# Weight tiles in two halves, read woven by the products of a two-layer hybrid encoder

## The chip, the cores and the metric

The kernel runs on one core of one Trainium2 chip. The metric is the device time of one execution in microseconds; the median of the runs is compared. Four engines matter here: TensorE (PE, its weight loads are called PEld), VectorE (DVE), ScalarE (ACT) and GpSimd (POOL). SyncE (SP) issues most of the DMA transfers.

## What is computed

Two layers act on 256 tokens of 2048 channels, all in float32. The reference, cut to what matters:

```python
def hybrid_layer(x, ...):
    h = rmsnorm(x, norm_g)
    proj = h @ w_in                                   # 2048 x 13376
    (c_a, c_glu, c_gate, q_down, kv_down, k_pe, m_gate, g_conv, g_mla) = jnp.split(proj, idx, axis=-1)
    # causal depthwise convolution of width 31, LayerNorm over channels, two gates
    y_conv = conv_branch(c_a, c_glu, c_gate, conv_w, conv_b, conv_ln_g, conv_ln_b) @ w_proj_conv
    # 16 heads, queries and keys from 512 latent channels, chunk-causal mask
    y_mla = mla_branch(q_down, kv_down, k_pe, m_gate, cos, sin, ..., w_uq, ..., w_ukv, ...) @ w_proj_mla
    y = jax.nn.sigmoid(g_conv) * y_conv + jax.nn.sigmoid(g_mla) * y_mla
    return x + y @ w_out
```

## The kernel before

**Products.** Every matrix product keeps a 128x128 block of the activations stationary in TensorE and lets a block of weights of up to 512 columns (384 or 320 for the low-rank inputs, `down`) move past it. For accuracy each float32 operand is split in two parts of the format fp32r, `hi` (rounded) and `lo` (the rest), and each product becomes three: activation `hi` by weight `hi`, activation `lo` by weight `hi`, activation `hi` by weight `lo`. The 256 tokens make two halves `t`, each with an accumulator `acc` in PSUM.

**Weight pieces.** The weights are cut into pieces of two blocks of 128 rows (`KS = 2`) by one block of columns. The host lays a piece out so that each partition has its two rows one after the other. SyncE loads a piece into `raw` (`load`, up to four pieces ahead), ScalarE copies it to `hi` (`split_hi`, three ahead), VectorE subtracts to get `lo` (`split_lo`, two ahead). The first two pieces of the program are loaded and split row by row. A full piece then serves twelve products of 512 columns: two rows, two halves of the tokens, three parts. `order_of_products` says in which order; `products_at_end` issues the last products of the program.

**Order.** `order_of_layer` lists the blocks of a layer: gated inputs of the convolution (`glu`), latent inputs (`down`), query and key/value products (`uq`, `ukv`) with the attention of eight pairs of heads between them, gates (`cgate`, `mgate`, `gmla`, `gconv`), the projections `pmla` and `pconv`, and `wout`. Each engine executes its instructions in the order in which the program issues them.

**The planner.** After each piece the program calls `background(n)`, which stands for one slot of time. The slot's length is a formula, and VectorE and ScalarE get a budget of it less the cost of the next split:

```python
slot = 12 * (n / 2400 + 0.0133) - 0.04
for e, split_us in (("vec", KS * n / 960 + 0.06), ("act", KS * n / 1066 + 0.04)):
    budget[e] = min(budget[e], 0.0) + slot - split_us
```

Evacuations of accumulators and attention steps come due at fixed slots and are charged. As long as VectorE's budget is positive, entries of the queue `fill` are issued: the 31 taps of the convolution for each of eight blocks (`conv`, tile `v_t`, running sum `s1c`), and then the LayerNorm (`mean`, `centre`, `var`, `factors`, `apply`) and the gating (`gated`), which yields `ycT`, the stationary operand of `pconv`. With budget left, ScalarE computes taps ahead (`assist`, tile `tap`). When `pconv` is reached, `run_fill` is called until `ycT` exists, and `before_pconv` forces each of its four parts before the pieces that use it.

Of the kernel before, what the change touches and what calls it, by code (L numbers as in the profile page):

```python
# [11 lines left out]
F32 = mybir.dt.float32  # L12
F32R = mybir.dt.float32r
# [6 lines left out]
P = 128  # L20
# [4 lines left out]
DEPTH = 2  # L25
# [32 lines left out]
R_QA, R_KVA, R_QR, R_KR, R_N = 0, LORA, 2 * LORA, 2 * LORA + ROPE, 2 * LORA + 2 * ROPE  # L58

KS = 2  # L60
N_WARM = 19


# [60 lines left out]
def trunk(ctx: ExitStack, tc: tile.TileContext, xT, x, g_in, pos, win, wuq, wukv, wpc, wpm, wo, cst, rows, invf, out):  # L124
# [19 lines left out]
    pe, vec, act, gps, sp = (InOrder(e) for e in (nc.tensor, nc.vector, nc.scalar, nc.gpsimd, nc.sync))  # L144
# [3 lines left out]
    raw_p = pool("raw", 5)  # L148
    split_p = pool("split", 3)
# [18 lines left out]
    pieces = []  # L168

    def plan(layer, stream):  # L170
        ap, nk = streams[stream]
        i, at = taken.get((layer, stream), (0, 0))
        n = blocks_of_layer()[stream][i]
        mine = []
        for g in range(nk // KS):
            size = P * KS * n
            pieces.append((ap[layer, at : at + size].rearrange("(p k c) -> p k c", p=P, k=KS), n))
            at += size
            mine.append(len(pieces) - 1)
        taken[layer, stream] = (i + 1, at)  # L180
        return nk, n, mine
# [6 lines left out]
    loaded, highs, done, blocks_begun = {}, {}, {}, [0]  # L188
    LOAD_AHEAD, HI_AHEAD, LO_AHEAD = 4, 3, 2

    def load(i):
        if i >= len(pieces) or i in loaded:
            return
        ap, n = pieces[i]
        loaded[i] = t = raw_p.tile([P, KS, n], F32, tag="raw", name=f"raw{i}")
        for a in range(0, KS, 1 if i < 2 else KS):
            k = slice(a, a + 1 if i < 2 else KS)
            sp.dma_start(t[:, k, :], ap[:, k, :])

    def split_hi(i):  # L200
        if i >= len(pieces) or i in highs:
            return
        load(i)
        highs[i] = split_p.tile([P, KS, pieces[i][1]], F32R, tag="hi", name=f"hi{i}", bufs=4)
        singly = i < 2
        for a in range(0, KS, 1 if singly else KS):
            k = slice(a, a + 1 if singly else KS)

            for step in ("h", "w"):
                if step == "w":  # L210
                    act.copy(highs[i][:, k], loaded[i][:, k])
                    if singly:
                        split_lo(i, k)
                elif i * KS < NCT:
                    for c in range(i * KS + k.start, i * KS + k.stop):
                        first_h(c)
        for a in range(1, LOAD_AHEAD + 1):
            load(i + a)

    def split_lo(i, k=slice(0, KS)):  # L220
        if i >= len(pieces) or done.get(i, (0, 0, 0))[2] >= k.stop:
            return
        lo = done[i][1] if i in done else split_p.tile([P, KS, pieces[i][1]], F32R, tag="lo", name=f"lo{i}")
        vec.tensor_sub(lo[:, k], loaded[i][:, k], highs[i][:, k].bitcast(F32))
        done[i] = highs[i], lo, k.stop


# [23 lines left out]

    def background(n):
        clock[0] += 1
        slot = 12 * (n / 2400 + 0.0133) - 0.04
        for e, split_us in (("vec", KS * n / 960 + 0.06), ("act", KS * n / 1066 + 0.04)):
            budget[e] = min(budget[e], 0.0) + slot - split_us
        while True:
            due = [e for e in steps if e[0] <= clock[0]]
            if not due:
                break  # L260
            steps[:] = [e for e in steps if e[0] > clock[0]]
            for _, costs, f in due:
                spend(costs)
                f()
            while early:
                early.pop(0)()
        while fill and budget["vec"] > 0:
            after, slots, scalar = fill[0][1]
            if after and clock[0] < marks.get(after, 1 << 30) + slots or scalar and budget["act"] < 0:
                break  # L270
            run_fill()

        while assist and budget["act"] > 0.8 and assist[0]():
            budget["act"] -= 0.85
        finish_late()
# [13 lines left out]
    def order_of_products(i, last, tardy):  # L289

        two = range(2)
        if i < 2:
            return [(t, kk, p) for kk in range(KS) for p in range(3) for t in two]
        high, low = (lambda t, p: [(t, kk, p) for kk in range(KS)]), (lambda t: [(t, kk, 2) for kk in range(KS)])
        if last:
            return high(0, 0) + high(0, 1) + high(1, 0) + low(0) + high(1, 1) + low(1)
        if tardy:
            return high(0, 0) + high(1, 0) + low(0) + low(1) + high(0, 1) + high(1, 1)  # L300
        return [e for t in two for p in two for e in high(t, p)] + low(0) + low(1)

    def products_at_end(last, n, pts, stat, evacuate, evacuate_half):

        own = s_p.tile([P, n // 2], F32, tag="s0", name="right_half")

        def issue(t, places, out, columns=slice(0, n), start=False, stop=False):
            todo = [(j, kk, p) for j in places for p in range(3) for kk in range(KS)]
            for at, (j, kk, p) in enumerate(todo):
                hi, lo, _ = done[last[j]]  # L310
                sh, sl = stat(NCT - KS * len(last) + j * KS + kk, t)
                stationary, w = ((sh, hi), (sl, hi), (sh, lo))[p]
                pe.matmul(out, stationary, w[:, kk, columns], start=start and at == 0, stop=stop and at == len(todo) - 1)

        half = n // 2
        issue(0, (0, 1), pts[0][:, :n], stop=True)
        evacuate(0, pts[0][:, :n])
        issue(1, (0,), pts[1][:, :n])
        issue(1, (1,), pts[1][:, :half], slice(0, half), stop=True)
        evacuate_half(0, pts[1][:, :half], True)  # L320
        evacuate_half(half, pts[1][:, half:n], False)
        issue(1, (1,), own, slice(half, n), start=True, stop=True)
        evacuate_half(half, own, True)

    def product(planned, stat, evacuate, evac_at=EVAC_AT, costs=(0.0, 0.0), before=None, tardy=None, final=None):
        nk, n, mine = planned
        blocks_begun[0] += 1
        pts = [acc_p.tile([P, 512], F32, tag=f"acc{blocks_begun[0] % 2}{t}", name=f"acc{mine[0]}_{t}") for t in range(T)]

        def evac():  # L330
            for t in range(T):
                evacuate(t, pts[t][:, :n])

        for j, i in enumerate(mine):
            for a in range(HI_AHEAD + 1):
                split_hi(i + a)
                if a <= LO_AHEAD:
                    split_lo(i + a)
            hi, lo, _ = done[i]
            if before:  # L340
                before(j)
            if final and j >= len(mine) - 2:
                if j == len(mine) - 1:
                    products_at_end(mine[-2:], n, pts, stat, evacuate, final)
                background(n)
                continue
            for t, kk, part in order_of_products(i, j == len(mine) - 1, j == tardy):
                k = j * KS + kk
                sh, sl = stat(k, t)
                stationary, w = ((sh, hi), (sl, hi), (sh, lo))[part]  # L350
                pe.matmul(
                    pts[t][:, :n], stationary, w[:, kk, :],
                    start=k == 0 and part == 0, stop=k == nk - 1 and part == 2,
                )
            if j == len(mine) - 1:
                steps.insert(0, (clock[0] + 1 + evac_at, costs, evac))
            background(n)
# [205 lines left out]
    for l in range(DEPTH):  # L563
# [712 lines left out]
        for kind, i, pl in planned:  # L1276
            if kind == "glu":
                at = EVAC_AT
                if i == 0 and l == 0:
                    at = 6  # L1280
# [58 lines left out]
def _blocked(w, widths):  # L1339

    k, at, out = w.shape[0] // (KS * P), 0, []
    for n in widths:
        b = w[:, at : at + n].reshape(k, KS, P, n).transpose(0, 2, 1, 3)
        out.append(b.reshape(-1))
        at += n
    return np.concatenate(out)
# [30 lines left out]
def _layout(inp):  # L1377
# [7 lines left out]
    for l in range(DEPTH):  # L1385
# [24 lines left out]
    rows_of = [np.arange(D), _rows()]  # L1410
    rows_of_w = {"wuq": _rows()[:LORA], "wukv": _rows()[:LORA]}
    g = np.stack([f("norm_g")[l][rows_of[l]] for l in range(DEPTH)])
    return {
        "xT": np.ascontiguousarray(x.reshape(SEQ, NCT, P).transpose(2, 1, 0)),
        "x": x.reshape(T, P, D),
        "g": np.concatenate([g.reshape(DEPTH * NCT, P).T, x.T[:P]], 1),
        "pos": np.ascontiguousarray(f("positions").reshape(T, P).T),
        "win": np.stack([_blocked(f("w_in")[l][rows_of[l]][:, cols], bl["win"]) for l in range(DEPTH)]),
        "wuq": both("w_uq", "wuq"),
        "wukv": both("w_ukv", "wukv"),  # L1420
        "wpc": both("w_proj_conv", "wpc"),
# [23 lines left out]
```

## Time and profile before

| what | value |
|---|---|
| median of 3 runs | 1875.94 us (1875.94 to 1876.02) |
| span of the profiled execution | 1875.0 us (first to last instruction) |
| time of that execution beside the span | the runs' 1875.94 us, 0.94 us more than the span |
| TensorE busy, matmuls | 1869.4 us, 8577 |
| VectorE busy | 1578.0 us (84%) |
| ScalarE busy | 1360.5 us (73%) |
| GpSimd busy | 495.7 us (26%) |
| moved by DMA | 445.05 MB, 237 GB/s in the mean |
| granted clock of TensorE | 1.000 |

Busy shares of TensorE say little, since matmuls overlap in its pipeline: a matmul's duration includes its way through the array. How far apart matmuls start is read from the chain of waits, whose pieces have a length and a count. A row of the groups has the tile written, the tiles read, the shapes, the count, the busy time and the mean duration in ns of one; a row of the chain has its start, its length and what it was; a row of the windows has the window, its length, each engine's busy time and count, the clock, the DMA share and GB/s.

### The profile page before, as it was taken

To read this page: it belongs to the slowest core of one execution; us is meant where nothing else is said; L and a number is where in the kernel's file an instruction comes from. 1 tells how busy PE (TensorE), PEld (TensorE's weight loads), DVE (VectorE), ACT (ScalarE), POOL (GpSimd) and SP (SyncE) were. 2 spreads that over 40 slices of the span, in tenths; PEclk is the share of its full clock that TensorE was granted. 3 is DMA by queue.
4 is the path that set the end of the run, shared out by engine and by line. 5 is a ranking of instruction groups with operands and counts; after the bars stand their busy time and mean duration, and the time that the engine had idled before them with its cause. 6 is when DMAs were issued, how large, how long until landed. Compare 5 with 4: busy or idle time off the path is not lost.

```text
span 1875.0 us, 27166 instructions
## 1 busy us (share of the span) xinstructions
PE 1869.4 (100%) x8577; PEld 1570.9 (84%) x8577; DVE 1578.0 (84%) x2453; ACT 1360.5 (73%) x2510; POOL 495.7 (26%) x942
## 2 busy tenths in 40 slices
PE   9999999999999999999999999999999999999999
PEld 8988888888888888888899888888888888888887
DVE  6899998898999988766679899889899999885664
ACT  7678888888888876644557688788889888574442
POOL 1055555542200000122221455555322000001210
PEclk9999999999999999999999999999999999999999
DMA  9688878787765566678876787887877556667775
GB/s 322 219 264 255 261 256 258 257 275 226 244 204 192 194 207 218 208 239 278 290 234 216 260 267 253 260 255 262 267 231 242 196 191 204 206 206 222 239 250 166
DMA packets 138960, 445.05 MB, mean 237 GB/s; under 512 B 23680, under 2 KB 29312, under 8 KB 138816
## 3 DMA queue, kind: packets, MB, share of 16 engines
q1 hardware_dynamic: 105120, 359.89, 59.2%
q0 software_dynamic: 32832, 82.62, 13.8%
q8 instruction: 67, 1.10, 0.2%
q10 hardware_dynamic: 864, 0.80, 0.1%
q14 instruction: 77, 0.63, 0.1%
HBM read 399.18 MB, written 44.04 MB: 236 GB/s over the span
## 4 chain that ended last, share of the span: by engine, by line
PE 99%; DMA 1%; DVE 0%; ACT 0%; SPq 0%; issue 0%; DVEq 0%
PE acc L135 96%; PE s L135 2%; PE o_ps L135 1%; DMA raw<-in_win 0%; DMA gx<-in_g 0%; DVE xres L135 0%; ACT hi L135 0%; PE var L135 0%; PE mu L135 0%; SPq L135 0%; DVEq L135 0%
## 5 line engine op out<-in xcount | busy, mean ns | idle before, releaser
L135 ACT CAST hi<-raw 128x1024 fp32r<-128x1024 f32 (+3 forms) x682 | 700.3, 1033 | 405.0 <-PE acc L135 348.9
L135 DVE TENSOR_TENSOR lo<-raw,hi 128x1024 fp32r<-128x1024 f32 (+3 forms) x682 | 814.0, 1195 | 191.5 <-PE acc L135 145.7
L135 PE MATMUL acc<-hi,hT 128*128 128x512 f32 (+2 forms) x1728 | 419.6, 382 | 0.0
L135 PEld LDWEIGHTS acc<-hi,hT 128*128 128x128 f32 x1728 | 319.6, 188 | 59.1
L135 PE MATMUL acc<-hi,h_hi 128*128 128x512 f32 (+2 forms) x864 | 260.5, 383 | 1.3 <-ACT hi L135 1.3
L135 PE MATMUL acc<-hi,h_lo 128*128 128x512 f32 (+2 forms) x864 | 260.1, 382 | 0.0
L135 ACT ACTIVATE tap<-u_t,cst 128x256 f32<-128x256 f32 x542 | 235.7, 501 | 2.8 <-DVE v_t L135 2.8
L135 PE MATMUL acc<-lo,h_hi 128*128 128x512 f32 (+2 forms) x864 | 229.7, 382 | 0.0
L135 PE MATMUL acc<-lo,hT 128*128 128x512 f32 (+2 forms) x864 | 229.3, 382 | 0.0
L135 DVE TENSOR_TENSOR v_t<-v_t,tap 128x512 f32<-128x512 f32 x271 | 186.4, 688 | 9.7 <-DVE v_t L135 0.9
L135 POOL DMA_DIRECT2D turned<-turn_d x88 | 49.4, 562 | 531.0 <-DVE v_t L135 315.0
L135 PEld LDWEIGHTS acc<-hi,h_lo 128*128 128x128 f32 x864 | 161.0, 188 | 30.1
L135 PEld LDWEIGHTS acc<-hi,h_hi 128*128 128x128 f32 x864 | 160.0, 188 | 30.9 <-ACT hi L135 2.2
L135 PEld LDWEIGHTS acc<-lo,h_hi 128*128 128x128 f32 x864 | 160.5, 188 | 30.2 <-DVE lo L135 0.3
L135 PEld LDWEIGHTS acc<-lo,hT 128*128 128x128 f32 x864 | 160.6, 188 | 29.9
L135 DVE SCALAR_TENSOR_TENSOR v_t<-u_t,cst,v_t 128x256 f32<-128x256 f32 x418 | 178.4, 480 | 2.0
L135 POOL DMA_DIRECT2D turn_d<-gate x184 | 100.5, 554 | 290.6 <-DVE gate L135 177.6
L135 PE MATMUL acc<-hi,ycT 128*128 128x512 f32 x512 | 127.8, 389 | 0.0
L135 PE MATMUL acc<-hi,oT 128*128 128x512 f32 x512 | 127.7, 389 | 0.0
L135 PE MATMUL acc<-hi,yT 128*128 128x512 f32 x512 | 127.5, 388 | 0.0
L135 PE MATMUL acc<-hi,qkc 128*128 128x512 f32 x448 | 115.4, 389 | 0.0
L135 PEld LDWEIGHTS acc<-hi,ycT 128*128 128x128 f32 x512 | 96.1, 188 | 20.0
(176 smaller groups left out, 2227.1 us busy)
## 6 DMA issues: line engine op xcount, KB each, us to landing
raw<-in_win SPq DMA_DIRECT2D x382, 512.0 KB, 4.2
raw<-in_wpm SPq DMA_DIRECT2D x64, 512.0 KB, 3.3
raw<-in_wpc SPq DMA_DIRECT2D x64, 512.0 KB, 4.2
raw<-in_wo SPq DMA_DIRECT2D x64, 512.0 KB, 4.9
raw<-in_wukv SPq DMA_DIRECT2D x32, 512.0 KB, 4.1
turned<-turn_d POOLq DMA_DIRECT2D x56, 256.0 KB, 4.7
raw<-in_win SPq DMA_DIRECT2D x32, 384.0 KB, 4.6
raw<-in_wuq SPq DMA_DIRECT2D x24, 512.0 KB, 4.3
```

Source lines behind the costliest of these rows:

```text
L135: ins = getattr(self.engine, name)(*a, **k)
```

## The change

A piece is laid out anew. Within a partition, all even columns of its rows come first and all odd columns after them (`h`, then row `k`, then column `c`), so column 2c and column 2c+1 of a row are `KS * n / 2` elements apart, 2 KB for 512 columns. The first two pieces (`SINGLE`), which are loaded row by row, have the two halves within each row, 1 KB apart. `woven` hands a product an access pattern that takes a column from the one half and a column from the other by turns, so that the moving operand passes in the old column order and the accumulators look as before. Tiles and transfers are declared flat. The slot formula of the planner gets another constant, 0.0028 in place of 0.0133.

```diff
+SINGLE = 2
...
+    def part_of(i, a, k):
+        return a[:, k.start * pieces[i][1] : k.stop * pieces[i][1]]
+
+    def woven(i, a, kk, columns=None):
+
+        if i < SINGLE:
+            a = part_of(i, a, slice(kk, kk + 1)).rearrange("p (h c) -> p c h", h=2)
+        else:
+            a = a.rearrange("p (h k c) -> p k c h", h=2, k=KS)[:, kk]
+        return a if columns is None else a[:, columns.start // 2 : columns.stop // 2]
...
-        loaded[i] = t = raw_p.tile([P, KS, n], F32, tag="raw", name=f"raw{i}")
-        for a in range(0, KS, 1 if i < 2 else KS):
-            k = slice(a, a + 1 if i < 2 else KS)
-            sp.dma_start(t[:, k, :], ap[:, k, :])
+        loaded[i] = t = raw_p.tile([P, KS * n], F32, tag="raw", name=f"raw{i}")
+        for a in range(0, KS, 1 if i < SINGLE else KS):
+            k = slice(a, a + 1 if i < SINGLE else KS)
+            sp.dma_start(part_of(i, t, k), part_of(i, ap, k))
...
-                    act.copy(highs[i][:, k], loaded[i][:, k])
+                    act.copy(part_of(i, highs[i], k), part_of(i, loaded[i], k))
...
-        vec.tensor_sub(lo[:, k], loaded[i][:, k], highs[i][:, k].bitcast(F32))
+        vec.tensor_sub(part_of(i, lo, k), part_of(i, loaded[i], k), part_of(i, highs[i], k).bitcast(F32))
...
-        slot = 12 * (n / 2400 + 0.0133) - 0.04
+        slot = 12 * (n / 2400 + 0.0028) - 0.04
...
-                pe.matmul(out, stationary, w[:, kk, columns], start=start and at == 0, stop=stop and at == len(todo) - 1)
+                pe.matmul(out, stationary, woven(last[j], w, kk, columns), start=start and at == 0, stop=stop and at == len(todo) - 1)
...
-                    pts[t][:, :n], stationary, w[:, kk, :],
+                    pts[t][:, :n], stationary, woven(i, w, kk),
...
-        b = w[:, at : at + n].reshape(k, KS, P, n).transpose(0, 2, 1, 3)
+        b = w[:, at : at + n].reshape(k, KS, P, n // 2, 2).transpose(0, 2, 4, 1, 3)
...
+    first = win[0, : SINGLE * P * KS * bl["win"][0]].reshape(SINGLE, P, 2, KS, -1)
+    first[...] = first.transpose(0, 1, 3, 2, 4).copy().reshape(first.shape)
```

More of the change, by code (lines that the diff above doesn't have):

```diff
@@ L176, in plan @@
             size = P * KS * n
-            pieces.append((ap[layer, at : at + size].rearrange("(p k c) -> p k c", p=P, k=KS), n))
+            pieces.append((ap[layer, at : at + size].rearrange("(p e) -> p e", p=P), n))
             at += size
@@ L203, in split_hi @@
         load(i)
-        highs[i] = split_p.tile([P, KS, pieces[i][1]], F32R, tag="hi", name=f"hi{i}", bufs=4)
-        singly = i < 2
+        highs[i] = split_p.tile([P, KS * pieces[i][1]], F32R, tag="hi", name=f"hi{i}", bufs=4)
+        singly = i < SINGLE
         for a in range(0, KS, 1 if singly else KS):
@@ L222, in split_lo @@
             return
-        lo = done[i][1] if i in done else split_p.tile([P, KS, pieces[i][1]], F32R, tag="lo", name=f"lo{i}")
-        vec.tensor_sub(lo[:, k], loaded[i][:, k], highs[i][:, k].bitcast(F32))
+        lo = done[i][1] if i in done else split_p.tile([P, KS * pieces[i][1]], F32R, tag="lo", name=f"lo{i}")
+        vec.tensor_sub(part_of(i, lo, k), part_of(i, loaded[i], k), part_of(i, highs[i], k).bitcast(F32))
         done[i] = highs[i], lo, k.stop
@@ L293, in order_of_products @@
         two = range(2)
-        if i < 2:
+        if i < SINGLE:
             return [(t, kk, p) for kk in range(KS) for p in range(3) for t in two]
@@ L1412, in _layout @@
     g = np.stack([f("norm_g")[l][rows_of[l]] for l in range(DEPTH)])
+    win = np.stack([_blocked(f("w_in")[l][rows_of[l]][:, cols], bl["win"]) for l in range(DEPTH)])
+    first = win[0, : SINGLE * P * KS * bl["win"][0]].reshape(SINGLE, P, 2, KS, -1)
+    first[...] = first.transpose(0, 1, 3, 2, 4).copy().reshape(first.shape)
     return {
@@ L1417, in _layout @@
         "pos": np.ascontiguousarray(f("positions").reshape(T, P).T),
-        "win": np.stack([_blocked(f("w_in")[l][rows_of[l]][:, cols], bl["win"]) for l in range(DEPTH)]),
+        "win": win,
         "wuq": both("w_uq", "wuq"),
```

## The prediction

> **What bounds the kernel now.** I read the page first, then the chain of waits that ended last, the waits of TensorE, the chain cut to windows, and the groups by shape. The page and the waits:
>
> ```profile
> span 1875.0 us, 27166 instructions
> PE 1869.4 (100%) x8577; PEld 1570.9 (84%) x8577; DVE 1578.0 (84%) x2453; ACT 1360.5 (73%) x2510; POOL 495.7 (26%) x942
> ...
> PE 99%; DMA 1%; DVE 0%; ACT 0%; SPq 0%; issue 0%; DVEq 0%
> ...
> PE acc L135 <- ACT hi L135: 1.3, 2, 0.9
> ```
>
> TensorE carries 99% of the last chain and waits 1.3 us in all. So the time is the number of products times their spacing; one microsecond off the products is one off the kernel, until another engine becomes late. The first and the last of the next rows are windows' groups, (x) being counts; the middle rows are the chain of waits, x products back to back:
>
> ```profile
> 0.00:1875.00 1875.00, 1820.79 (x8160) 1515.42 (x8160) 58.46 (x120) 137.31 (x492) 1.00 0.73 237
> ...
> 470.86 231.23 PE acc L135 x1020
> ...
> 30.05 29.29 PE acc L135 x169
> ...
> 61.94 14.10 PE acc L135 x96
> ```
>
> There are 8160 products into `acc` at granted clock 1.00. Those of 512 columns (470.86 on) come every 231.23/1020 = 226.7 ns, those of 384 (30.05 on) every 29.29/169 = 173.3, those of 320 (61.94 on) every 14.10/96 = 146.9. From 384 to 512 columns is 53.4 ns for 128, so 0.417 ns a column: 512 columns stream in 213.3 ns, and 13.3 are left over; 384 leave 13.3 and 320 leave 13.5. Each product loses the same 13.3 ns, whatever its length. 8160 x 13.3 = 108.5 us is the most that any change of reading can win.
>
> Is it a fixed charge of the instruction? The groups by shape give durations, which hold the streaming time plus one constant latency:
>
> ```profile
> L135 PE MATMUL acc<-hi,hT 128*128 128x512 f32 x1536 | 383.6, 389 | 0.0
> L135 PE MATMUL acc<-hi,hT 128*128 128x320 f32 x64 | 10.8, 309 | 0.0
> L135 PE MATMUL o_ps<-pv,qk_t 128*128 128x256 f32 x8 | 2.3, 282 | 0.0
> L135 PE MATMUL o_ps<-pv 128*128 128x128 f32 x24 | 5.3, 221 | 0.0
> L135 PE MATMUL s<-qk_t 128*128 128x128 f32 x32 | 7.1, 222 | 0.0
> L135 PEld LDWEIGHTS acc<-hi,hT 128*128 128x128 f32 x1728 | 319.6, 188 | 59.1
> ```
>
> 512 against 320 columns is 80 ns, against 256 it is 107: both 0.417 a column, so these lose alike. From 256 to 128 columns the duration falls by 60 or 61 ns where the columns account for 53.3. The short products lose 7 ns less, about half of the 13.3. A charge for issue would not shrink; a loss that runs for as long as the next weights are loaded beside the stream (one load of 128 columns for each product) would. So I read the 13.3 ns as the moving stream giving way while it reads, not as overhead of the instruction.
>
> **The change part by part.** (1) The weave. All 8160 `acc` products read their moving tile as pairs, one column from each half of the tile; for 512 columns the halves are 2 KB apart, for the first two pieces 1 KB. The count, the weight loads, the columns written and their order stay. No product in the trace alternates its reads column by column, so the effect is bounded from both sides: on the good side the whole 13.3 ns goes; on the bad side the stream needs extra steps, priced under the rivals. Nearest rows: the 128-column products, which leave 13.3 - 7 = 6 ns. The planner's new constant puts 2.8 ns in place of 13.3; that is an input of the change and no evidence, but it names a size between the 6 of the row and 0. I take 2.8: asking two places by turns gives each twice the time between its reads, which is what a stream that must give way now and then lacks. Gain 10.5 x 8160 = 85.7 us, with 6 ns left 7.3 x 8160 = 59.6.
>
> [...]
>
> (2) Tiles declared flat, splits and loads on flat slices: the same 128x1024 casts and subtractions and the same 512 KB transfers, so nothing. The host's reordering lies outside the time.
>
> (3) Weight transfers come 4.6% closer together:
>
> ```profile
> SPq L135 <- DVE lo L135: 1377.5, 595, 6.8
> ...
> 0.00:50.00 50.00, 47.92 (x239) 43.17 (x240) 32.50 (x65) 35.76 (x62) 5.08 (x14) 1.00 0.91 319
> ...
> 900.00:950.00 50.00, 50.00 (x223) 41.40 (x222) 33.67 (x51) 28.95 (x52) 15.69 (x30) 1.00 0.89 288
> ```
>
> SyncE's queue waits for `lo`, that is for a free buffer, not for data. The busiest stretch after the start moves 288 GB/s, which becomes 302, below the 319 of the first 50 us. I cost it at nothing; if that cover fails, some 2 to 5 us around 900 to 950.
>
> (4) The planner's slot, the part that costs. `background` budgets VectorE per piece: 12 x (512/2400 + 0.0133) - 0.04 = 2.680 us before, 2.554 after, 0.126 less. The split is charged 2 x 512/960 + 0.06 = 1.127, so 1.553 were left for evacuations and fill (the convolution and LayerNorm), and 1.427 remain. VectorE's own occupation and the times of the fill:
>
> ```profile
> 67.00:450.00 383.00, 383.00 (x1793) 321.88 (x1792) 343.38 (x614) 317.23 (x699) 186.35 (x356) 1.00 0.79 255
> 450.00:690.00 240.00, 240.00 (x1063) 198.87 (x1063) 230.76 (x312) 201.66 (x350) 17.62 (x32) 1.00 0.66 212
> ...
> L135 DVE TENSOR_SCALAR v_t<-u_t,cst x32: 403/409/418, 67.3 to 1552.8; 128x256 f32<-128x256 f32 x32
> ...
> L135 DVE TENSOR_TENSOR s1c<-s1c,v_t x2: 692/692/692, 644.2 to 690.4; 128x512 f32<-128x512 f32 x2
> ...
> L135 PE MATMUL acc<-hi,ycT x256: 389/389/389, 765.0 to 851.3; 128*128 128x512 f32 x128
> L135 DVE TENSOR_TENSOR ycT<-v_t,ycT x8: 683/686/695, 749.5 to 776.9; 128x512 fp32r<-128x512 f32 x8
> ...
> 390.07 1.89 PE s L135 x16
> 391.96 8.19 PE acc L135 x36
> 401.30 24.50 PE acc L135 x108
> ...
> 709.26 1.29 DVE L135 TENSOR_TENSOR v_t<-v_t,ln_stats 128x512 f32<-128x512 f32 x2
> 710.59 1.23 DVE L135 TENSOR_TENSOR lo<-raw,hi 128x1024 fp32r<-128x1024 f32 x1
> ...
> 729.63 1.22 DVE L135 TENSOR_TENSOR lo<-raw,hi 128x1024 fp32r<-128x1024 f32 x1 [1.50 <-PE acc L135]
> ...
> 746.20 1.23 DVE L135 TENSOR_TENSOR lo<-raw,hi 128x1024 fp32r<-128x1024 f32 x1
> 749.47 1.29 DVE L135 TENSOR_TENSOR ycT<-v_t,ycT 128x512 fp32r<-128x512 f32 x2 [2.04 <-ACT ycT L135]
> ```
>
> Layer 0: the taps run from 67.3 to 690.4 us with fill always waiting, VectorE 230.76 of 240 us busy towards the end. Less seven interludes of attention (scores 1.89 us from 390.07, values 1.15 us up to 401.30, 3 us a pair) these are 602/2.72 = 221 slots. They lose 221 x 0.126 = 27.8 us of budget, 27.8/1.427 = 19.5 slots, about one more for ScalarE's assisted taps, whose budget shrinks alike. Between the last tap and `pconv`, the first product of `ycT`, lie (765.0 - 690.4)/2.72 = 27.4 slots; 7 are left, so `pconv` is reached where the old run stood at 709: centring. There `run_fill` is forced. Of the 41 us from 709 to the first `ycT` pair's end at 750.8, some 17 are splits (14 from 710.59 to 746.20) and 5 idle (the gaps before 729.63 and 749.47 the longest); 19 us of work and about 5 of hops between engines must run while TensorE waits. VectorE is two pieces ahead, 5 us, so the stall is 19. The other three parts of `ycT` took from 751 to 777, with ten splits among them, so 13 us of their own; beside six splits they need 20 us, and six pieces of the new spacing last 15.6: 5 more. Layer 0: 24 us.
>
> ```profile
> L135 DVE TENSOR_SCALAR v_t<-u_t,cst x2: 411/412/412, 1056.3 to 1056.6; 128x256 f32<-128x256 f32 x2
> ...
> L135 DVE TENSOR_TENSOR s1c<-s1c,v_t x3: 691/692/694, 1506.6 to 1596.2; 128x512 f32<-128x512 f32 x3
> ...
> L135 PE MATMUL acc<-hi,ycT x256: 389/389/389, 1697.2 to 1783.5; 128*128 128x512 f32 x128
> ...
> 1659.89 1.30 DVE L135 TENSOR_TENSOR ycT<-v_t,ycT 128x512 fp32r<-128x512 f32 x2 [2.05 <-ACT ycT L135]
> ```
>
> Layer 1 is full only from 1056.3: (540 - 18)/2.72 = 192 slots lose 24.2 us, 18 slots with the assists, of the 36.8 between 1596.9 and 1697.2. `pconv` then begins where the old run stood at 1648, 13 us before the first pair's end at 1661.2, half of it splits: a stall of 2, and 4 for the other parts. Sum of both layers 30 us; bounds 0 (the slot waits inside the tail are skipped when forced, the costs are generous) and 45.
>
> The sum: span 1875.0 and 0.94 around it make the median 1875.94. 1875.94 - 85.7 + 30 = **1820.2 us**. With no stall 1790; with 6 ns left and 45 us of stalls 1861. The likeliest case's own range is 1784 to 1862.
>
> **The rivals.** *The gain is smaller and the stalls take most of it:* with 4 to 7 ns gained (33 to 57 us) and 40 of stalls, 1859 to 1883, here counted from 1862. The products' spacing of 220 to 223 ns would show it.
>
> *The loss belongs to the weight load and the weave changes nothing.* For it: each product has such a load, and the loss is alike at 320 and 512 columns. Against it: it is the moving stream that loses the steps. The spacing stays 226.7, the planner still defers, and the forced tails come: 1876 + 30 = 1906, between 1896 and 1916.
>
> *The weave makes the stream slower, which is the other side.* Its place is every `acc` product; its price, one extra step of 0.417 ns a column, is 213 ns each, 1.7 ms in all and about 3.6 ms of time; one step every second column gives 2.7 ms. It decides early: with 30 us of stalls the change loses from 3.7 ns less gain a product, a spacing above 226.7 - 3.7 = 223.0 ns. Against it: the contiguous stream loses 13.3 ns for 320 columns as for 512, so moving on through memory is not what it pays for.
>
> [...]
>
> **How the numbers follow.** The likeliest case 0.80, the small gain eaten 0.06 (half of it faster, a third the same), no effect 0.05, the slower stream 0.09. The range 1784 to 1880 holds the first, less a twentieth, and most of the second: 0.81. A measurement of this kernel tells 0.2%, 3.75 us, from no change. Faster 0.83, same 0.02, slower 0.15.
>
> **What would show it.** The chain's products of 512 columns should read near 216 ns apart (x1020 in 220 us), their mean duration fall from 389 to near 378. TensorE's waits should rise from 1.3 us to some 30, nearly all on `ycT` at the two starts of `pconv`, the larger in layer 0. The first `ycT` subtraction of layer 0 should still come near 750 us, in layer 1 near 1615. VectorE's busy time should stay within 1% of 1578. The prediction is wrong if the spacing stays at 226.7 or grows, or if `pconv` starts without a wait.

## The result: no difference that can be measured

The changed kernel takes 1875.18 us (median of 12 runs) against 1876.24 before, ratio 0.9995 with a 95% interval of 0.9987 to 1.0004. The prediction was 1820. The profiled execution has a span of 1873.0 us. Its page, with the slices of TensorE, of its granted clock and of VectorE:

```profile
span 1873.0 us, 27021 instructions
PE 1803.1 (96%) x8577; PEld 1587.0 (85%) x8577; DVE 1587.8 (85%) x2526; ACT 1295.7 (69%) x2363; POOL 492.7 (26%) x942
...
PE   9999999999999995599999999999999999976999
...
DVE  6898988899999998567679999889999999875664
...
PEclk9999999999999998799999999999999999988999
...
PE 92%; DVE 4%; ACT 2%; DMA 1%; POOL 1%; issue 1%; DVEq 0%; SPq 0%; ACTq 0%; POOLq 0%
```

TensorE, full in every slice before, now falls to half in two slices of layer 0 and to six or seven tenths in two of layer 1; the clock dips with it, to eight and seven tenths in layer 0 and eight in layer 1, and VectorE, ScalarE and GpSimd enter the last chain (4, 2 and 1%). The waits of TensorE, then the chain, first in the stretch without waits, then around the two starts of `pconv` (the rows at 792.42 and 1717.26 go to the ends of their windows, 800 and 1745 us):

```profile
PE acc L136 <- ACT ycT L136: 51.4, 8, 11.6
PE var L136 <- DVE parts L136: 12.8, 1, 12.8
...
448.53 279.72 PE acc L136 x1296
...
753.94 7.33 PE acc L136 x24
765.85 8.19 PE acc L136 x24
779.81 8.04 PE acc L136 x24
792.42 7.72 PE acc L136 x28
...
1677.67 7.97 PE acc L136 x24
1690.21 8.51 PE acc L136 x24
1704.49 8.21 PE acc L136 x24
1717.26 27.88 PE acc L136 x121
```

The weave does what the forecast said: 1296 products in 279.72 us is one every 215.8 ns, where it was 226.7. On 8160 products that is 10.9 x 8160 = 89 us. They are given back at the two starts of `pconv`. TensorE waits 64.2 us there, on `ycT` eight times and once on the variance. And the products after each wait are slow: the six groups of 24 take 48.3 us where 24 products at 215.8 ns take 5.2, 31.1 in all, so 17 us more. Behind the last wait of each layer, 28 products take 7.72 us and 121 take 27.88, where the spacing gives 6.04 and 26.11: 3.4 us more. Waits and slow products make 85 of the 89 us.

### The profile page after: what moved, and what is told of

Same layout as the page of the kernel before. It is cut to its first block, busy times and chain, and to the rows that moved or that the text cites. A ratio compares the mean times of both kernels' runs of the same rounds, so it can differ in the third digit from the quotient of the medians.

```text
span 1873.0 us, 27021 instructions
## 1 busy us (share of the span) xinstructions
PE 1803.1 (96%) x8577; PEld 1587.0 (85%) x8577; DVE 1587.8 (85%) x2526; ACT 1295.7 (69%) x2363; POOL 492.7 (26%) x942
## 4 chain that ended last, share of the span: by engine, by line
PE 92%; DVE 4%; ACT 2%; DMA 1%; POOL 1%; issue 1%; DVEq 0%; SPq 0%; ACTq 0%; POOLq 0%
PE acc L136 90%; PE s L136 1%; DVE v_t L136 1%; PE o_ps L136 1%; DVE lo L136 1%; ACT hi L136 1%; DVE ln_stats L136 1%; POOL rsq_t L136 0%; DVE turned L136 0%; DVE rsq_t L136 0%; DMA raw<-in_win 0%; ACT ycT L136 0%; ACT L136 0%; DMA gx<-in_g 0%; POOL turn_d L136 0%
## 5 line engine op out<-in xcount | busy, mean ns | idle before, releaser
L136 PE MATMUL acc<-hi,hT 128*128 128x512 f32 (+2 forms) x1728 | 401.1, 372 | 0.9 <-ACT junk L136 0.5
L136 PE MATMUL acc<-hi,h_hi 128*128 128x512 f32 (+2 forms) x864 | 251.9, 373 | 0.4 <-ACT hi L136 0.4
L136 PE MATMUL acc<-hi,h_lo 128*128 128x512 f32 (+2 forms) x864 | 251.4, 373 | 0.0
L136 DVE SCALAR_TENSOR_TENSOR v_t<-u_t,cst,v_t 128x256 f32<-128x256 f32 x564 | 242.9, 479 | 4.5
L136 PE MATMUL acc<-lo,h_hi 128*128 128x512 f32 (+2 forms) x864 | 220.5, 372 | 0.0
L136 PE MATMUL acc<-lo,hT 128*128 128x512 f32 (+2 forms) x864 | 220.2, 372 | 0.0
L136 PE MATMUL acc<-hi,ycT 128*128 128x512 f32 x512 | 137.5, 414 | 51.4 <-ACT ycT L136 51.4
L136 ACT ACTIVATE tap<-u_t,cst 128x256 f32<-128x256 f32 x396 | 179.0, 499 | 0.3 <-DVE v_t L136 0.3
L136 PEld LDWEIGHTS acc<-hi,ycT 128*128 128x128 f32 x512 | 105.7, 208 | 72.1 <-ACT ycT L136 54.5
L136 DVE TENSOR_TENSOR v_t<-v_t,tap 128x512 f32<-128x512 f32 x198 | 135.5, 685 | 1.5 <-DVE v_t L136 0.5
```

Source lines behind the costliest of these rows:

```text
L136: ins = getattr(self.engine, name)(*a, **k)
```

## Experiments

Each kernel is compared with the kernel before, run beside it. The two halves of the change first: the weave alone, and the planner's constant alone.

**e1_weave_old_slot**

```diff
-        slot = 12 * (n / 2400 + 0.0028) - 0.04
+        slot = 12 * (n / 2400 + 0.0133) - 0.04
```

> The woven reads with the planner's old constant 0.0133. Theory A (the weave wins 10.8 ns on each of 8160 products, 88 us; the smaller slot budget pushes LayerNorm behind the start of pconv, where TensorE waits and its clock falls): the fill is planned as before, so pconv finds ycT nearly ready; VectorE, full from 450 to 690 us and from 1380 to 1602, cannot follow the faster products there, so no gain in these 460 us and 4.7% of the other 1415: about 1810 us, between 1800 and 1830, with the waits on lo spread in small pieces and the clock near 1.00. Theory B (VectorE's whole work before pconv sets the time, whatever the planner does): 1870 to 1880 us.

Measured: 1798.69 us, ratio 0.9586 (0.957 to 0.9602). With the old constant the weave is worth 78 us. Its page and waits:

```profile
span 1796.3 us, 27166 instructions
PE 1785.8 (99%) x8577; PEld 1571.8 (88%) x8577; DVE 1565.9 (87%) x2453; ACT 1345.1 (75%) x2510; POOL 495.1 (28%) x942
...
PE acc L136 <- DVE lo L136: 1.7, 5, 0.5
```

No wait on `ycT` is left and TensorE stands at 99% again. This is lower than the 1800 I set as its bound: VectorE followed the faster products in its full stretches better than I thought (1104 products from 450 to 690 us, where the kernel before has 1063). Theory B falls, since the same work of VectorE fits into 1799 us.

**e2_new_slot_only**

```diff
-        slot = 12 * (n / 2400 + 0.0133) - 0.04
+        slot = 12 * (n / 2400 + 0.0028) - 0.04
```

> Contiguous reads as before, only the planner's constant is the new 0.0028. Theory A: products 226.7 ns apart, and the same late LayerNorm as in the changed kernel: the time of before plus the waits at both pconv starts and the cold clock, 1876 + 60 to 85 = 1935 to 1960 us. Theory B: within 10 us of 1876.

Measured: 1960.99 us, ratio 1.0451 (1.043 to 1.0471). That is 1 us above the range I gave. The constant alone costs 84.5 us, and the waits of TensorE are those of the changed kernel, almost to the tenth:

```profile
PE acc L135 <- ACT ycT L135: 51.3, 8, 11.6
PE var L135 <- DVE parts L135: 12.8, 1, 12.8
```

A gain of 78 to 89 us and a loss of 84.5 make the measured zero. The next kernel takes the lateness away in another manner.

**e4_weave_22_taps**

```diff
-            for k in range(CONV_W):
+            for k in [*range(TAPS - 1), CONV_W - 1]:
```

> The changed kernel with 22 of the 31 taps of the convolution (nine taps left out), so VectorE has some 58 us less fill in each layer. Theory A: LayerNorm is done before pconv in both layers, no waits, clock 1.00: 1876 - 88 = 1788 us, 1783 to 1795. Theory C (something else, such as the weight transfers or the clock, takes the gain back): 1820 us or more, with waits elsewhere than at pconv.

Measured: 1789.43 us, ratio 0.9536 (0.9517 to 0.9555), with the new constant 0.0028. With less fill ahead of it, the tail is in time, and 87 of the 89 us of the weave remain. The transfers, which are as close together as in the changed kernel, take at most the other 2. e1, which has all the taps, is 9 us above this kernel; where these lie is not taken apart here.

**e8_force_before_splits** asks why the waits are twice what I had reckoned.

```diff
         for j, i in enumerate(mine):
+            if before:
+                before(j)
             for a in range(HI_AHEAD + 1):
                 split_hi(i + a)
...
-            if before:
-                before(j)
```

> The changed kernel (constant 0.0028), with the forced rest of the fill at pconv issued ahead of the piece's splits instead of behind them. Claim: in the changed kernel the three later waits on ycT in each layer (4.6, 5.8, 4.6 us) come from VectorE's order: a lo split that must wait for TensorE's products stands ahead of the fill. With the fill ahead of the splits it runs beside the products: these waits fall to 0 to 3 us each and the clock drops less, 1845 to 1862 us. If instead the fill's own work sets the waits: 1870 to 1878.

Measured: 1853.55 us, ratio 0.9877 (0.9861 to 0.9894). The waits of TensorE in layer 0, from 700 to 800 us:

```profile
PE acc L136 <- ACT ycT L136: 17.5, 4, 10.7
PE var L136 <- DVE parts L136: 12.8, 1, 12.8
```

The first wait stays (10.7 after 11.6); the other three fall from 15.0 us to 6.8 together. Over both layers the waits on `ycT` fall from 51.4 us to 33.6. So the later waits came in the main from the order on VectorE. In the changed kernel the timeline shows it (start, length, engine, what, and in brackets the idle time before and its end):

```profile
725.75 1.22 DVE L136 TENSOR_TENSOR lo<-raw,hi 128x1024 fp32r<-128x1024 f32 x1 [1.36 <-PE acc L136]
...
728.08 0.40 PE L136 MATMUL mu<-parts,ones 128*128 128x256 f32 x2
728.52 0.42 DVE L136 COPY ln_stats<-mu 128x256 f32<-128x256 f32 x1 [1.54 <-PE mu L136]
...
753.94 3.78 PE L136 MATMUL acc<-hi,ycT 128*128 128x512 f32 x8 [11.61 <-ACT ycT L136]
...
774.12 1.22 DVE L136 TENSOR_TENSOR lo<-raw,hi 128x1024 fp32r<-128x1024 f32 x1 [1.52 <-PE acc L136]
775.27 1.28 DVE L136 TENSOR_TENSOR v_t<-v_t,ln_stats 128x512 f32<-128x512 f32 x2
...
779.81 3.78 PE L136 MATMUL acc<-hi,ycT 128*128 128x512 f32 x8 [5.78 <-ACT ycT L136]
```

At 774.12 a `lo` split has just waited for TensorE to finish with a buffer; only behind it come the fill's `v_t` and, 5.7 us after the split's start, the first product on `ycT`. VectorE and TensorE take turns where I had them side by side. The first forced stretch of layer 0 loses its lead in another way. It begins with the copy of `mu`, and `mu` is a product of TensorE itself, which stands in TensorE's queue behind its last products before `pconv` (728.08). So VectorE starts at 728.5 with no lead at all, and e8, which moves only the splits, leaves this wait at 12.8 us.

**e10_pe_kept_busy** prices the clock: products of zeros stand in the waits.

```diff
+    def keep_busy(n):
+        idle = s_p.tile([P, 256], F32, tag="s0", name="idle")
+        for i in range(n):
+            pe.matmul(idle, zeros[:, :P], zeros, start=i == 0, stop=i == n - 1)
...
                 mark("mean")
+                if l == 0:
+                    keep_busy(100)
...
             finish_late()
+            if j % 2 == 0:
+                keep_busy(36 if j else 80)
```

> The changed kernel (constant 0.0028) with products of zeros, 256 columns of 120 ns each, issued into the waits at pconv: 100 after mean in layer 0, 80 ahead of the first and 36 ahead of the other three parts of ycT. They take no longer than the waits they stand in (12.8, about 10 and 4.6 us). If the lower granted clock after these waits costs what the chain shows (the 24 products after each take 7.3 to 8.2 us instead of 5.2, about 17 us in all), the time falls to 1857 to 1864 us with the clock near 1.00; if the clock costs nothing, 1873 to 1880.

Measured: 1861.36 us, ratio 0.9918 (0.9901 to 0.9934): 13.8 us less than the changed kernel, by products that compute nothing. The first page row below is the clock of the changed kernel, by slices, the second that of this one:

```profile
PEclk9999999999999998799999999999999999988999
```

```profile
PEclk9999999999999999999999999999999999999999
```

The waits of the changed kernel at the two starts of `pconv` are 4.6 us and longer. Its granted clock is 0.63 to 0.74 over the six groups of 24 products, and 0.70 in the mean from 728 to 793 us (the row below):

```profile
728.00:793.00 65.00, 25.63 (x79) 19.70 (x78) 43.47 (x75) 29.86 (x44) 2.19 (x4) 0.70 0.25 81
```

Behind shorter waits the clock fell too. In e8 it is 0.77 in the 7.3 us behind a wait of 2.0 us (the rows below). In this kernel two of the eight groups, behind waits of 1.75 us that the zeros did not fill, also run at 0.77 and 0.76, so the zeros do not win back all the time of the slow products. Behind a wait of 1.6 us in e8 (the products at 763.17) the clock stayed at 1.00.

```profile
1696.30 2.86 PE L136 MATMUL acc<-hi,ycT 128*128 128x512 f32 x8 [1.99 <-ACT ycT L136]
...
1696.30:1703.57 7.27, 7.24 (x25) 5.75 (x26) 3.63 (x4) 2.65 (x4) 0.00 (x0) 0.77 0.25 82
```

Three kernels look for a better setting of the woven kernel.

**e6_weave_slot_0105** (constant 0.0105 in place of 0.0028)

> The woven reads with the planner's constant 0.0105, between the two. Theory A: VectorE lags less behind the products than with 0.0133 (1798.7 us), while LayerNorm ends some 5 slots later; with 14 us of slack before pconv in layer 0 about half of the 10 us above the floor are won if the slack holds: 1794 us, 1790 to 1800. If the tail comes too late in layer 0: 1800 to 1815.

**e9_weave_slot_0155** (constant 0.0155)

> The woven reads with a larger constant, 0.0155. Constants of 0.0028, 0.0105 and 0.0133 gave 1875, 1820 and 1799 us. If the rest above the floor (1789 us with 22 taps) is still lateness of the tail, 1792 to 1798; if it is VectorE's lag behind the products in the full stretches, more fill per slot makes it worse: 1799 to 1806.

**e7_weave_more_assist** (constant 0.0133, and `budget["act"] > 0.3` in place of `> 0.8` in the line of `assist`)

> The woven reads with the old constant 0.0133, and ScalarE takes a tap ahead when 0.3 us of its budget are left rather than 0.8. Each tap it takes saves VectorE about 0.2 us. Theory A with VectorE as what is late: 30 more taps in a layer, 6 us less on VectorE, 1793 to 1798 us. If ScalarE's casts become late instead: over 1800.

Measured: 0.0105 gives 1819.61 us (ratio 0.9696, 0.9681 to 0.971), with four waits on `ycT` of 17.9 us; 0.0155 gives 1804.76 (0.962, 0.9606 to 0.9634); more assists 1802.13 (0.9609, 0.9595 to 0.9623). My hope for 0.0105 was wrong: its time lies above both ranges I gave, and the slack before `pconv` that I counted on does not cover the later tail. More assists miss the range I hoped for as well; TensorE waits longer on `lo` (3.5 us, 1.7 in e1) and no longer on ScalarE's `hi` (1.4 in both). Below 0.0133 the tail is late. At 0.0155 TensorE waits 4.7 us on `lo`, 3.0 more than in e1, which is only half of the 6 us lost against it. e1 stays the best version, 1798.69 us, faster than both kernels by 4.1%.

The last two ask what the weave does inside TensorE.

**e3_reads_by_kind**: tiles as before, another order of reading for some blocks.

```diff
-                    pts[t][:, :n], stationary, w[:, kk, :],
+                    pts[t][:, :n], stationary, moving(w, kk),
...
+        ("gmla", 0): ("(c h) -> h c", dict(h=2)),
+        ("pmla", 2): ("(b h c) -> b c h", dict(h=2, c=4)),
```

> The kernel before, its tiles laid out as before, but some blocks read their moving columns in another order (so the columns of those blocks come out permuted or from the other row; that part of the computation is changed). Spacing of 512-column products by block. Theory A1 (any read that alternates between two places hides the 13.3 ns): 216 ns for halves by turns (mgate 1), rows by turns (mgate 2), four by turns (mgate 3), and 226.7 for two runs of 256 (gmla 3). Theory A2 (it is the form of the access pattern, two dimensions, that matters): two runs also 216. Theory A3 (the stream must not stay in one small place: distance decides): by turns at 64 B and less (pmla 0 to 3) stays at 226.7 while 128 B and more gives 216. [...]

The chain gives start, length and number of products for each block (rows in the order of the table below):

```profile
444.83 20.29 PE acc L135 x94
...
482.90 21.25 PE acc L135 x75
...
509.58 35.64 PE acc L135 x79
...
552.96 37.37 PE acc L135 x81
...
596.60 33.63 PE acc L135 x78
...
639.94 15.19 PE acc L135 x67
...
699.90 15.11 PE acc L135 x70
...
721.86 15.19 PE acc L135 x67
...
744.86 25.16 PE acc L135 x74
...
780.00 16.25 PE acc L135 x65
...
815.83 19.51 PE acc L135 x40
...
910.71 34.36 PE acc L135 x79
```

| how 512 columns are read | ns for one product |
|---|---|
| two places by turns, 1 or 2 KB apart (halves, or rows) | 215.9 |
| four places by turns | 283 |
| every second column, evens then odds | 451 |
| every fourth column | 461 |
| every eighth column | 431 |
| two runs of 256 | 226.7 |
| two places by turns, 16 bytes apart | 215.9 |
| two places by turns, 8 bytes apart (columns 0, 2, 1, 3) | 226.7 |
| two columns from each of two places by turns | 340 |
| four columns from each of two places by turns | 250 |
| eight places by turns | 488 |
| sixteen places by turns | 435 |

Theory A1 holds for two places down to 16 bytes, and fails for four, which it had at 216. The form of the access pattern is not what matters (two runs stay at 226.7), and of A3 only 8 bytes is left. The slow rival was true of the neighbours of this change: four places, or steps of two columns, take 283 and 451 ns a product in place of 226.7.

**e5_short_weight_loads**

```diff
+                m = loads.get(tuple(now), P) if part and k < nk - 1 else P
                 pe.matmul(
-                    pts[t][:, :n], stationary, w[:, kk, :],
+                    pts[t][:m, :n], stationary[:, :m], w[:, kk, :],
```

> The kernel before with contiguous reads; in the first two blocks of gmla and of gconv the products with the activation's low part and with the weight's low part keep only 64 (block 0) or 32 (block 1) of the 128 stationary columns, save the last row of blocks, so the correction of the other tokens is left out there. Theory L (the 13.3 ns are lost to the next weights' load, one load of 128 columns each): a product followed by a load of 64 columns loses 6.7 ns, of 32 columns 3.3: spacing 220.0 and 216.7 instead of 226.7. Theory S (the contiguous stream alone loses them): 226.7 everywhere.

The chain in the block with loads of 64 columns and in that with 32 (one product in three keeps 128):

```profile
504.81 18.36 PE acc L135 x80
...
527.79 17.29 PE acc L135 x75
```

18.36/80 = 229.5 ns and 17.29/75 = 230.5, where contiguous products with full loads have 226.7: shorter loads win nothing. The loss of 13.3 ns does not follow the length of the weight load, and what I made of the 128-column products in the prediction falls with that. Why one stream of fp32r columns loses 13.3 ns a product and two streams by turns lose 2.5 stays open; only that it is so is shown.

## Why the prediction was wrong

**The weave** (step 1) was right: 10.9 ns a product, 89 us, where I took 10.5 and 85.7. The expected duration of 378 ns came as 379. The reason I gave is not borne out: by e5 the loss does not follow the weight load, and why reading from two places by turns avoids it stays open.

**Splits, transfers and VectorE's work** (steps 2 and 3) cost nothing that shows, as forecast; e4 leaves at most 2 us for the transfers, and VectorE's busy time rose by 0.6%.

**The planner's slot** (step 4) had the right mechanism and sign, and this is where the sum broke: 30 us were forecast, 84.5 are measured (e2). Term by term:

| term | forecast, us | measured, us |
|---|---|---|
| first wait, layer 0 | 19 | 24.4 (12.8 and 11.6) |
| first wait, layer 1 | 2 | 9.9 |
| later parts of `ycT`, layer 0 | 5 | 15.0 |
| later parts of `ycT`, layer 1 | 4 | 15.0 |
| slow products after the waits | 0 | 20.5 |

The rows below are, in the changed kernel, TensorE's first products on `ycT` in layer 1 with the wait before them, the last tap sum of each layer, and ScalarE's taps:

```profile
1677.67 3.78 PE L136 MATMUL acc<-hi,ycT 128*128 128x512 f32 x8 [9.93 <-ACT ycT L136]
...
L136 DVE TENSOR_TENSOR s1c<-s1c,v_t x3: 692/693/693, 621.6 to 715.2; 128x512 f32<-128x512 f32 x3
...
L136 DVE TENSOR_TENSOR s1c<-s1c,v_t x3: 693/694/696, 1527.9 to 1622.9; 128x512 f32<-128x512 f32 x3
...
L136 ACT ACTIVATE tap<-u_t,cst 128x256 f32<-128x256 f32 x396 | 179.0, 499 | 0.3 <-DVE v_t L136 0.3
```

The delay of the taps itself was nearly right. In layer 0 the products before `pconv` end at 728.3, (728.3 - 715.9)/2.59 = 4.8 slots after the last tap, where I had 7; in layer 1 they end at 1677.67 - 9.93 = 1667.7, 17 slots after it instead of 19. Part of the two slots is the assists: ScalarE's tap rows fell from 542 to 396, two to a tap, so 73 taps fewer. The planner charges VectorE 0.08 us more for each, about two slots a layer, where I had put one.

The step that failed is the next one: "VectorE is two pieces ahead, 5 us", and for the later parts "beside six splits they need 20 us, and six pieces of the new spacing last 15.6: 5 more". Both let VectorE work ahead of TensorE or beside it. In layer 0 the lead was nothing, because the forced work began with `mu`, which TensorE itself delivers: 24.4 us of waiting for 19. Behind each later part's `lo` split, which must wait for its buffer, VectorE started only when TensorE had finished; with the fill ahead of the splits the later waits of layer 0 are 6.8 us (e8), near the 5 forecast, and the kernel is 22 us faster. In layer 1 the two slots count too: `pconv` was reached when VectorE stood at the factors of LayerNorm, which the old run began at 1641 and not 1648. And the clock behind the waits, 0.70 in the mean from 728 to 793 us, was not in the sum at all; e10 won 14 us by it.

The first `ycT` of layer 0 came at 753.9, near the 750 I named, but that of layer 1 at 1677.7 instead of 1615. By the sum's own terms `pconv` of layer 1 begins at 1697.2 - 77.6 + 24 = 1644 (10.5 ns on each of the 7392 products ahead of it); the figure of 1615 left out the 24 us of layer 0. The rest is what the waits cost above the forecast. The measured terms add up to 85 us, as much as the constant costs in e2.

The rival "the gain is smaller and the stalls take most of it" named the right loser for the wrong reason, a smaller gain. Its range of 1859 to 1883 us holds the measured time, but its sign, a spacing of 220 to 223 ns, did not come, so that hit was luck. What I should have priced is a rival with the full gain and the waits unhidden.

## What to carry to other kernels

When the bound engine gets faster, everything that was planned in units of its time moves as well: check what a hand-written schedule will do with the new number before entering it, since here the true number cost 76 us against leaving the old one. Work forced in front of a waiting engine overlapped with nothing here where something ahead of it in its queue waited for that same engine (15.0 us of later waits in layer 0, 6.8 in e8), or where its input came from that engine (12.8 us). And a wait of TensorE had a second price, in the products behind it: in the changed kernel after each of the eight waits on `ycT` of 4.6 to 11.6 us (six groups of 24 products took 7.3 to 8.5 us in place of 5.2), in e8 after one of 2.0 us, in e10 after two of 1.75 us.

## What the hardware showed that was not expected

Moving fp32r columns read from two places by turns took 215.8 ns for 512 columns in the changed kernel and 215.9 in e3, there also with the places only 16 bytes apart: 2.5 ns above the 213.3 that 0.417 ns a column make, where one contiguous run took 226.7, 13.3 ns above them. In e3 four places by turns took 283 ns, eight 488, sixteen 435, and every second, fourth or eighth column 431 to 461. So the order of reading alone won 5% of a product's time here, or more than doubled it.

The granted clock fell behind waits of TensorE as short as 2.0 us (e8) and 1.75 us (e10): the products behind such a wait ran at 0.76 to 0.77, and in e8 they took 7.3 us where 24 at 215.8 ns take 5.2.
